# A down projection in parts: 24 of its 44 inner tiles as seven products of sums, partial results accumulated in DRAM

## The chip, the cores and the metric

The kernel runs on one core of a Trainium2 chip. The metric is the device time in microseconds (us) of one execution; less is better. The engines are called by their names in the profile as well: TensorE (PE; its weight loads are PEld), VectorE (DVE), ScalarE (ACT), GpSimd (POOL) and SyncE (SP), whose queue issues most DMAs.

## What is computed

One step of a decoder layer for 512 prompt tokens and 64 sample tokens, 576 together. Cut to what matters here:

```
x = x + concat(A, B) @ w_out                       # 2048 -> 2048
up = rmsnorm(x, g_ffn) @ w_up                      # 2048 -> 2 x 5632
upc = causal_dwconv(up_ext, w_dw_f, b_dw_f)        # width 3, along the tokens
x = x + (silu(upc[..., :D_FF]) * upc[..., D_FF:]) @ w_down     # 5632 -> 2048
gate = sigmoid(rmsnorm(x, g_ple) @ w_ple_gate)
x = x + gate * (p @ w_ple_proj)
```

All is float32. The down projection is the product with `w_down`: 44 inner tiles of 128 channels (`NF`), 16 output tiles (`KT`).

## The kernel before

Channels lie on the 128 partitions and tokens along the free axis, as two halves of 288 (`HT`). A float32 product is made of three matmuls in the format `fp32r`: every operand is split into a high part `h` and a rest `l`, and `wh x bh + wh x bl + wl x bh` is summed in PSUM. So a tile of weights (128x128) against all 576 tokens is six matmuls of 288 columns (L862, L864, L866).

Weights come in one stream, `wstream`, in the order in which TensorE wants them: units of 8 tiles, 512 KB each, in five buffers `raw`. A piece is 4 tiles (128x512). `prepare` splits a piece: ScalarE copies the high part into `wh` (L249), VectorE subtracts it and leaves the rest in `wl` (L250), four buffers each, up to four pieces ahead of TensorE.

The up projection (`up_pair`, one pair of output tiles for each of 44 `j`) is already computed by seven products of sums (Strassen's scheme in Winograd's form): instead of eight block products of (output row) x (inner half) x (token half) it takes seven, in the order of `PRODS`, with sums of weight pieces made on VectorE (`add_up`, L209), sums of operands made once (`sum_in`), and the seven results put together by subtractions from PSUM (L718) and copies on ScalarE. A piece there feeds 12 matmuls, in a plain product 24.

Each pair's result then goes through a convolution of width 3, SiLU and a product (`conv_f`, `hidden`), mostly on VectorE: that gives the hidden tile `j`. For the 22 `j` in `SOON` this is done beside the next pair of the up projection and the hidden tile is stored in DRAM (`hidd`); for the 22 in `LATER` the raw result is stored (`upd`) and the convolution is done beside the down projection. Such side work is dealt out from the queues `todo` and `urgent` after every fourth tile, at a rate (`state["rate"]`) that the phases set; the scheduler of the tile framework then orders the instructions of each engine.

The down projection runs over four chunks of 12, 10, 16 and 6 inner tiles (`CHUNKS`, in `ORDER`). In each, the first three output tiles are computed together and the other 13 one after the other; the three accumulators (`acc`, two PSUM banks each) rotate. At the end of an output's chunk VectorE adds its accumulator to `x1r`, the running sum in SBUF, which is loaded from DRAM (`x1d`) when the down projection begins (L810, L905). In the last chunk the sum is normalised, split and squared for the next product (`split_in`, `add_square`). Each chunk's hidden tiles are fetched beside the chunk before (`fetch_hidden`), the first chunk's at the end of the up projection (L721 to L724).

Of the kernel before, what the change touches and what calls it, by code (L numbers as in the profile page):

```python
# [39 lines left out]
SOON = sorted([*range(2, NF - 3, 2), NF // 4, 3 * NF // 4])  # L40
LATER = [j for j in range(NF) if j not in SOON]
ORDER = SOON + LATER
CHUNKS = [12, 10, 16, 6]

COMING = [12, 22, 34, 44, 44]
RATE_D = [0.3, 1.6, 1.0, 0.0]
# [17 lines left out]
def plan():  # L64
# [46 lines left out]
    at = 0  # L111
    for c, n in enumerate(CHUNKS):
        js = ORDER[at : at + n]
        at += n
# [34 lines left out]
def trunk_kernel(ctx: ExitStack, tc: tile.TileContext, A, O):  # L149
# [28 lines left out]
    HID = [x for n in (2, 3, 4, 0, 1) for x in by_kind[n]] + SPARE  # L178
    RES2 = by_kind[5] + by_kind[6]
# [48 lines left out]
    def prepare(s):  # L228
# [17 lines left out]
        else:  # L246
            h = tl([P, SUB * P], HID[32 + 2 * spare], f"wh{s}", dt=F32R)
            l = tl([P, SUB * P], HID[33 + 2 * spare], f"wl{s}", dt=F32R)
# [327 lines left out]
    def sum_in(q):  # L576

        box = {}
        return [(1.5, lambda: add_in(q, box)), (1.1, lambda: first_in(q, box)), (1.4, lambda: last_in(q, box))]

    def add_in(q, box):
        g = []
        for n in range(2):
            g.append(tmp(f"xg{2 * q + n}"))
            nc.scalar.activation(g[n], res[2 * q + n], AF.Copy, scale=v("g_ffn", 2 * q + n))
        e, o = g
        ta, tb = tmp(f"ta{q}"), tmp(f"tb{q}")
        nc.vector.tensor_tensor(out=ta[:, 0, :], in0=e[:, 0, :], in1=e[:, 1, :], op=ALU.subtract)
        nc.vector.tensor_tensor(out=ta[:, 1, :], in0=o[:, 1, :], in1=ta[:, 0, :], op=ALU.add)
        nc.vector.tensor_tensor(out=tb[:, 0, :], in0=e[:, 1, :], in1=o[:, 1, :], op=ALU.subtract)  # L590
        nc.vector.tensor_tensor(out=tb[:, 1, :], in0=o[:, 0, :], in1=ta[:, 1, :], op=ALU.subtract)
        box.update(e=e, o=o, ta=ta, tb=tb)

    def first_in(q, box):
        e = box["e"]
# [474 lines left out]
```

## Time and profile before

| | |
|---|---|
| median of 3 runs | 2446.71 us (2446.13 to 2448.26) |
| the profiled execution, its own time | 2449.88 us |
| its span in the trace | 2448.1 us |
| PE busy | 2422.2 us, 99% |
| PEld busy | 2412.7 us, 99% |
| DVE busy | 1804.1 us, 74% |
| ACT busy | 1115.7 us, 46% |
| POOL busy | 92.5 us, 4% |
| matmuls | 18200 |
| mean granted TensorE clock | 0.996 of full speed |

The span is that of the instructions in the trace; the execution's own time lies 1.8 us above it. The busy share of an engine is the time in which it had an instruction under way; matmuls are pipelined, so a busy PE may still be short of its best pace.

### The profile page before, as it was taken

The numbers are of one execution on the slowest core, as the hardware profiler recorded it, in microseconds if no ns is written. First come the engines' busy times: TensorE is split into PE (matmuls) and PEld (weight loads), VectorE is DVE, ScalarE is ACT, GpSimd is POOL, SyncE is SP. The second block draws the span as 40 slices with busy tenths as digits, with TensorE's granted clock in tenths as the row PEclk, the third lists the DMA queues.
The fourth block names the chain that finished last, engine by engine and source line by source line (L and its number), as shares of the span: only waits on it lengthen the run. The fifth ranks groups of instructions, "written<-read, shape, count | busy, mean of one in ns | idle before, by whom it ended". The sixth has DMA issues, their size and how long they took to land.

```text
span 2448.1 us, 45485 instructions
## 1 busy us (share of the span) xinstructions
PE 2422.2 (99%) x18200; PEld 2412.7 (99%) x18200; DVE 1804.1 (74%) x3155; ACT 1115.7 (46%) x2072; POOL 92.5 (4%) x175
## 2 busy tenths in 40 slices
PE   9999999999999999999999999999999999999997
PEld 8999999999999999999999999999999999999997
DVE  7877788885888879888888798886459762254445
ACT  6444445433665545445445454454235431243334
POOL 1000000000200000000000000000000000000000
PEclk9999999999999999999999999999999999999998
DMA  6332222333563333433333434357334432222322
GB/s 238 95 84 83 85 84 84 123 107 101 193 216 118 115 121 99 132 111 110 118 118 115 121 98 132 112 172 275 101 110 148 133 120 79 86 87 78 121 96 93
DMA packets 106196, 294.71 MB, mean 120 GB/s; under 512 B 23568, under 2 KB 27792, under 8 KB 105984
## 3 DMA queue, kind: packets, MB, share of 16 engines
q1 hardware_dynamic: 96096, 259.20, 33.8%
q0 software_dynamic: 9744, 32.60, 3.8%
q8 instruction: 143, 2.34, 0.4%
q14 instruction: 69, 0.57, 0.1%
q10 hardware_dynamic: 144, 0.01, 0.0%
HBM read 255.43 MB, written 36.32 MB: 119 GB/s over the span
## 4 chain that ended last, share of the span: by engine, by line
PE 95%; issue 2%; DMA 1%; DVE 1%; ACT 1%; POOL 0%; SPq 0%; DVEq 0%; POOLq 0%
PE acc L862 18%; PE acc L866 18%; PE acc L864 18%; PE acc_up L729 13%; PE acc_up L730 13%; PE acc_up L731 13%; POOL x1d L901 0%; DMA x<-in_xT 0%; PE vps L512 0%; DMA xs<-x1d 0%; PE mps L550 0%; PE acc L936 0%; PE acc L935 0%; PE acc L937 0%; DMA hq<-hidd 0%
## 5 line engine op out<-in xcount | busy, mean ns | idle before, releaser
L249 ACT ACTIVATE wh<-raw 128x512 fp32r<-128x512 f32 x792 | 500.2, 632 | 945.1 <-PE acc L864 676.8
L250 DVE TENSOR_TENSOR wl<-raw,wh 128x512 fp32r<-128x512 f32 x792 | 543.5, 687 | 362.1 <-ACT wh L249 357.7
L729 PE MATMUL acc_up<-sx,wh 128*128 128x288 f32 x2464 | 726.8, 295 | 0.1
L731 PE MATMUL acc_up<-sx,wl 128*128 128x288 f32 x2464 | 726.6, 295 | 0.2 <-DVE wl L250 0.2
L730 PE MATMUL acc_up<-sx,wh 128*128 128x288 f32 x2464 | 726.5, 295 | 0.0
L729 PEld LDWEIGHTS acc_up<-sx,wh 128*128 128x128 f32 x2464 | 463.8, 188 | 0.8 <-ACT sq L303 0.3
L730 PEld LDWEIGHTS acc_up<-sx,wh 128*128 128x128 f32 x2464 | 463.8, 188 | 0.1
L731 PEld LDWEIGHTS acc_up<-sx,wl 128*128 128x128 f32 x2464 | 463.0, 188 | 0.4 <-DVE wl L250 0.4
L862 PE MATMUL acc<-xh,wh 128*128 128x288 f32 x1984 | 427.2, 296 | 5.7 <-ACT wh L249 5.3
L864 PE MATMUL acc<-xl,wh 128*128 128x288 f32 x1984 | 423.6, 295 | 0.3 <-DVE xl L291 0.3
L866 PE MATMUL acc<-xh,wl 128*128 128x288 f32 x1984 | 423.5, 294 | 0.0
L862 PEld LDWEIGHTS acc<-xh,wh 128*128 128x128 f32 x1984 | 318.4, 188 | 7.9 <-ACT wh L249 5.3
L864 PEld LDWEIGHTS acc<-xl,wh 128*128 128x128 f32 x1984 | 319.2, 188 | 0.8 <-DVE xl L291 0.6
L866 PEld LDWEIGHTS acc<-xh,wl 128*128 128x128 f32 x1984 | 318.1, 188 | 0.3 <-issue 0.3
L862 PE MATMUL acc<-hh,wh 128*128 128x288 f32 x1408 | 301.2, 295 | 2.3 <-DVE ua L718 1.8
L866 PE MATMUL acc<-hh,wl 128*128 128x288 f32 x1408 | 301.3, 295 | 0.0
L864 PE MATMUL acc<-hl,wh 128*128 128x288 f32 x1408 | 301.1, 295 | 0.0
L862 PEld LDWEIGHTS acc<-hh,wh 128*128 128x128 f32 x1408 | 226.6, 188 | 2.9 <-DVE ua L718 2.1
L864 PEld LDWEIGHTS acc<-hl,wh 128*128 128x128 f32 x1408 | 226.7, 189 | 0.0
L866 PEld LDWEIGHTS acc<-hh,wl 128*128 128x128 f32 x1408 | 226.3, 188 | 0.0
L249 ACT ACTIVATE wh<-sy 128x512 fp32r<-128x512 f32 x176 | 111.7, 635 | 160.6 <-PE acc_up L730 156.8
L445 DVE SCALAR_TENSOR_TENSOR cv<-ep,vec,cv 128x512 f32<-128x512 f32 x240 | 178.8, 745 | 0.0
(192 smaller groups left out, 2184.0 us busy)
## 6 DMA issues: line engine op xcount, KB each, us to landing
raw<-in_wstream SPq DMA_DIRECT2D x395, 512.0 KB
uz<-upd SPq DMA_DIRECT2D x44, 288.0 KB
upd<-ub POOLq DMA_DIRECT2D x22, 288.0 KB, 2.6
upd<-ua POOLq DMA_DIRECT2D x22, 288.0 KB, 2.4
hidd<-hp POOLq DMA_DIRECT2D x22, 288.0 KB, 3.9
hq<-hidd SPq DMA_DIRECT2D x22, 288.0 KB
x<-in_xT SPq DMA_DIRECT2D x16, 288.0 KB
xr<-in_xT SPq DMA_DIRECT2D x16, 288.0 KB
```

The costliest lines, as they stand in the source:

```text
L249: nc.scalar.activation(h, src, AF.Copy)
L250: nc.vector.tensor_tensor(out=l, in0=src, in1=h.bitcast(F32), op=ALU.subtract)
L445: tc.keep_in_program_order(nc.vector.scalar_tensor_tensor(out=cp, in0=halves(ep[:, k : k + SEQ]), scalar=w, in1=cp, op0=ALU.mult, op1=ALU. ...
L729: nc.tensor.matmul(place[prod], wh, bh, start=k == 0 and not on, stop=False, skip_group_check=on)
L730: nc.tensor.matmul(place[prod], wh, bl, start=False, stop=False, skip_group_check=on)
L731: nc.tensor.matmul(place[prod], wl, bh, start=False, stop=k == KT // 2 - 1, skip_group_check=on)
L862: nc.tensor.matmul(accs[n][:, h, :HT], wh, bh[:, h, :], start=st, stop=False)
L864: nc.tensor.matmul(accs[n][:, h, :HT], wh, bl[:, h, :], start=False, stop=False)
L866: nc.tensor.matmul(accs[n][:, h, :HT], wl, bh[:, h, :], start=False, stop=sp)
```

## The change

24 of the 44 inner tiles of the down projection go through the seven products as well. The down projection has seven parts (`DOWN`): plain ones with 6, 5, 5 and 4 inner tiles, and between them three parts of 8 inner tiles each by seven products (`quad1`, `quad3`, `quad5`). In such a part a block (`down_four`) is four output tiles by eight inner tiles: output row x inner half x token half, for two pairs of output tiles and four pairs of inner tiles. The weight sums are those of the up projection (`add_up`), the operand sums are made as `sum_in` makes them (`sum_steps`, in `fetch_two`).

Results no longer stay in SBUF between the parts: a plain part's accumulator is copied by ScalarE into one of four staging tiles and GpSimd adds it to `x1d` in DRAM by an accumulating DMA (L1000, L1001); a block's four result tiles are added in halves of the tokens, eight DMAs a block (L761). `x1d` is read back for the last part alone (L903). `LATER` is cut from 22 `j` to 8, so 36 pairs of the up projection have their convolution beside the next pair.

```diff
-SOON = sorted([*range(2, NF - 3, 2), NF // 4, 3 * NF // 4])
-LATER = [j for j in range(NF) if j not in SOON]
+LATER = [0, 1, NF // 3, NF // 2, 2 * NF // 3, NF - 3, NF - 2, NF - 1]
+SOON = [j for j in range(NF) if j not in LATER]
 ORDER = SOON + LATER
-CHUNKS = [12, 10, 16, 6]
-
-COMING = [12, 22, 34, 44, 44]
-RATE_D = [0.3, 1.6, 1.0, 0.0]
+DOWN = [(False, SOON[:6]), (True, SOON[6:14]), (False, LATER[:4] + SOON[14:15]), (True, SOON[15:23]),
+        (False, LATER[4:7] + SOON[23:25]), (True, SOON[25:33]), (False, LATER[7:] + SOON[33:])]
+
+RATE_D = [1.9, 0.0, 1.9, 0.0, 1.6, 0.0, 0.0]
...
+    for c, (summed, js) in enumerate(DOWN):
+        if summed:
+            for m in range(0, KT, 4):
+                add(f"quad{c}", "w_down", range(m, m + 4), js)
+            continue
...
+        elif phase.startswith("quad"):
+            w, m = outs[0]
+            for row, odd in ((0, 0), (1, 0), (1, 1), (0, 1)):
+                tiles += [(w, k, m + 2 * pair + row) for pair in range(2) for k in ks[odd::2]]
+            pieces += [(n // UNIT, prod, half) for prod in PRODS for half in range(2)]
...
+    def fetch(c):
+
+        summed, js = DOWN[c]
+        if summed:
+            return [f for n in range(0, len(js), 2) for f in fetch_two(c, js[n], js[n + 1])]
+        return [f for j in js for f in fetch_hidden(j, grab(c, 2))]
+
+    def fetch_two(c, i, j):
+        box = []
+
+        def load():
+            for m in (i, j):
+                box.append(tmp(f"hq{m}"))
+                nc.sync.dma_start(box[-1], hid_d[m])
+
+        return [(0.0, load)] + sum_steps(lambda: box, grab(c, 7), f"h{i}", sums_h.setdefault(c, []))
...
+    def down_four(c, ms):
+
+        ones, sixes, fives = (psum.tile([P, 2, 512], F32, tag="acc", name=f"acc{c}_{ms[0]}_{n}", bufs=3)
+                              for n in range(3))
+        place = {1: ones, 2: ones, 6: sixes, 7: sixes, 4: sixes, 5: fives, 3: fives}
+        o11, o12, o21, o22, first, u = (tl([P, 2, HT], STAGE[n], f"o{c}_{ms[0]}_{n}") for n in range(6))
+
+        def out(o, row, half):
+            for pair in range(2):
+                nc.gpsimd.dma_start(x1_d[ms[2 * pair + row]][:, half, :], o[:, pair, :], accum_op=ALU.add)
+
+        for prod in PRODS:
+            on = prod not in (1, 6, 5)
+            for pair in range(2):
+                dst = place[prod][:, pair, :HT]
+                for k, two in enumerate(sums_h[c]):
+                    wh, wl = weights()
+                    bh, bl = two[prod]
+                    end = k == len(sums_h[c]) - 1
+                    nc.tensor.matmul(dst, wh, bh, start=k == 0 and not on, stop=False, skip_group_check=on)
+                    nc.tensor.matmul(dst, wh, bl, start=False, stop=False, skip_group_check=on)
+                    nc.tensor.matmul(dst, wl, bh, start=False, stop=end, skip_group_check=on)
+                deal()
+            acc = place[prod][:, :, :HT]
+            if prod == 1:
+                nc.scalar.activation(first, acc, AF.Copy)
+            if prod == 6:
+                sub(u, acc, first)
+            if prod == 7:
+                sub(o22, acc, first)
+                sub(o22, o22, fives[:, :, :HT])
+                out(o22, 1, 1)
+            if prod == 2:
+                nc.scalar.activation(o11, acc, AF.Copy)
+                out(o11, 0, 0)
+            if prod == 4:
+                sub(o21, acc, first)
+                out(o21, 1, 0)
+            if prod == 3:
+                sub(o12, acc, u)
+                out(o12, 0, 1)
...
-                state["rate"] = 1.1
-                for i in ORDER[: COMING[0]]:
-                    urgent.extend(fetch_hidden(i, slot_of(i)))
+                state["rate"] = 0.8
+                urgent.extend(fetch(0))
...
-                nc.vector.tensor_tensor(out=res[m], in0=acc[:, :, :HT], in1=res[m], op=ALU.add)
-                if phase == n_down:
+                if phase != n_down:
+                    a = tl([P, 2, HT], STAGE[m % 4], f"o{phase}_{m}")
+                    nc.scalar.activation(a, acc[:, :, :HT], AF.Copy)
+                    nc.gpsimd.dma_start(x1_d[m], a, accum_op=ALU.add)
+                else:
+                    nc.vector.tensor_tensor(out=res[m], in0=acc[:, :, :HT], in1=res[m], op=ALU.add)
```

How the instructions stand on the engines is shown at three places; the number behind an underscore at a name's end is a buffer's.

TensorE, before, inside the first chunk of the down projection (`acc117_0` to `_2` are its first three accumulators, `hh` and `hl` hidden tiles, `x2` the two halves of the tokens): the four tiles of weight piece 818.

```order
L862 MATMUL acc117_2_19963<-hh6_19760,wh818_19910 128x288 x2
L864 MATMUL acc117_2_19963<-hl6_19761,wh818_19910 128x288 x2
L866 MATMUL acc117_2_19963<-hh6_19760,wl818_19911 128x288 x2
L862 MATMUL acc117_0_19961<-hh8_19766,wh818_19910 128x288 x2
L864 MATMUL acc117_0_19961<-hl8_19767,wh818_19910 128x288 x2
L866 MATMUL acc117_0_19961<-hh8_19766,wl818_19911 128x288 x2
```

TensorE now, at the start of the first part by seven products (`acc1_0_0` is the accumulator `ones` of its first block, `sxh8`, `sxh10` the operand sums of the pairs of hidden tiles 8, 9 and 10, 11):

```order
L771 MATMUL acc1_0_0_21216<-sxh8_2_20255,wh840_21123 128x288
L772 MATMUL acc1_0_0_21216<-sxh8_2_20255,wh840_21123 128x288
L773 MATMUL acc1_0_0_21216<-sxh8_2_20255,wl840_21124 128x288
L771 MATMUL acc1_0_0_21216<-sxh10_2_20338,wh840_21123 128x288
L772 MATMUL acc1_0_0_21216<-sxh10_2_20338,wh840_21123 128x288
L773 MATMUL acc1_0_0_21216<-sxh10_2_20338,wl840_21124 128x288
```

A tile of weights has three matmuls there, and twice as many pieces pass for the same number of matmuls.

VectorE, before, where the up projection hands over to the down projection (`ua43` is the last result of the up projection, `hl` the rests of hidden tiles, `wl817` to `wl819` weight pieces of the first chunk):

```order
L250 TENSOR_TENSOR wl817_19881<-raw276_19661,wh817_19880 128x512
L683 TENSOR_TENSOR hl28_20065<-hq28_20062,hh28_20064 128x576
L683 TENSOR_TENSOR hl30_20101<-hq30_20098,hh30_20100 128x576
L250 TENSOR_TENSOR wl818_19911<-raw277_19845,wh818_19910 128x512
L683 TENSOR_TENSOR hl32_20135<-hq32_20132,hh32_20134 128x576
L718 TENSOR_TENSOR ua43_19606<-acc_up2_7937,uu43_19609 128x288
```

VectorE now, where the first part by seven products hands over to the second plain part (`o1_12_2` and `o1_12_1` are the last two results of its last block, `sxh20` and `sxh23` operand sums of the next such part, `wl897` and `wl898` weight pieces of the plain part):

```order
L616 TENSOR_TENSOR sxh20_6_22412<-hq21_22370,sxh20_5_22411 128x576
L750 TENSOR_TENSOR o1_12_2_22025<-acc1_12_1_22021,o1_12_4_22027 128x576
L261 TENSOR_TENSOR wl897_22246<-raw304_22080,wh897_22245 128x512
L616 TENSOR_TENSOR sxh23_6_22477<-hq24_22463,sxh23_5_22476 128x576
L261 TENSOR_TENSOR wl898_22264<-raw305_22220,wh898_22263 128x512
L616 TENSOR_TENSOR sxh23_4_22475<-tah23_22465,sxh23_3_22474 128x576
L750 TENSOR_TENSOR o1_12_1_22024<-acc1_12_2_22022,o1_12_5_22028 128x576
```

The last subtraction of a part stands behind two weight pieces and two operand sums, as `ua43` stood behind hidden tiles. That place occurs after the first and the second such part; after the third only weight pieces stand there.

GpSimd, before, from the end of the up projection to the end of the program: stores of the up projection's results, and rows of the convolution's history.

```order
L749 DMA upd87_225<-ub43_19607 128x576
L748 DMA upd43_224<-ua43_19606 128x576
L624 MEMSET hist5_21967 128x12x2
L671 DMA out_ffn_conv<-last3_16371 128x216
L624 MEMSET hist6_22582 128x12x2
```

GpSimd now, from the last outputs of the first plain part (`odown0`) into the first block (`o1_0`):

```order
L1001 DMA x1d14_142<-odown0_14_21169 128x576
L1001 DMA x1d15_143<-odown0_15_21213 128x576
L761 DMA x1d1_129<-o1_0_3_21222 128x288
L761 DMA x1d3_131<-o1_0_3_21222 128x288
L761 DMA x1d0_128<-o1_0_0_21219 128x288
L761 DMA x1d2_130<-o1_0_0_21219 128x288
```

GpSimd has 144 accumulating DMAs there, one after the other, where it had almost nothing to do.

## Rows read from the trace of the kernel before

**Rows 1.** The page: the span, and busy time, share and instructions of each engine.

```profile
span 2448.1 us, 45485 instructions
...
PE 2422.2 (99%) x18200; PEld 2412.7 (99%) x18200; DVE 1804.1 (74%) x3155; ACT 1115.7 (46%) x2072; POOL 92.5 (4%) x175
```

**Rows 2.** Waits of PE: total us, times, longest us.

```profile
PE acc L862 <- ACT wh L249: 5.8, 2, 5.3
...
PE acc L862 <- DVE ua L718: 1.8, 1, 1.8
```

**Rows 3.** Windows: stretch, length, busy us of PE, PEld, DVE, ACT, POOL; PEclk, DMA.

```profile
1015.00:1616.20 601.20, 601.20 (x4538) 601.20 (x4537) 507.27 (x880) 298.59 (x567) 22.94 (x44) 1.00 0.37 118
...
2000.00:2060.00 60.00, 60.00 (x456) 60.00 (x455) 16.00 (x25) 12.04 (x19) 0.00 (x0) 1.00 0.25 80
...
1660.50:2224.30 563.80, 561.52 (x4228) 560.87 (x4227) 321.73 (x520) 212.12 (x435) 3.76 (x10) 1.00 0.39 122
...
1661.00:1700.00 39.00, 37.16 (x269) 36.92 (x268) 21.19 (x35) 14.65 (x30) 0.54 (x1) 0.96 0.82 290
```

**Rows 4.** Groups by line, PE, 1660.5 to 2224.3; L864 and L866 alike.

```profile
L862 PE MATMUL acc<-hh,wh 128*128 128x288 f32 x1408 | 301.2, 295 | 2.3 <-DVE ua L718 1.8 <-ACT wh L249 0.4
```

**Rows 5.** Timeline of PE: start us, us, instruction, count [idle before, releaser].

```profile
1664.09 0.53 PE L862 MATMUL acc<-hh,wh 128*128 128x288 f32 x2 [1.84 <-DVE ua L718]
...
1665.36 0.69 PE L864 MATMUL acc<-hl,wh 128*128 128x288 f32 x2
1665.84 0.69 PE L866 MATMUL acc<-hh,wl 128*128 128x288 f32 x2
...
1982.75 0.50 PE L862 MATMUL acc<-hh,wh 128*128 128x288 f32 x2 [0.44 <-ACT wh L249]
1983.09 0.42 PE L864 MATMUL acc<-hl,wh 128*128 128x288 f32 x2
1983.35 0.43 PE L866 MATMUL acc<-hh,wl 128*128 128x288 f32 x2
```

**Rows 6.** The chain that ended last, 1655 to 1665 us: start, us, what.

```profile
1655.56 5.48 DMA hq<-hidd
...
1663.66 0.38 DVE ua L718
```

**Rows 7.** Windows, columns as in rows 3: three pairs with a convolution, one without.

```profile
926.00:948.20 22.20, 22.20 (x169) 22.20 (x169) 20.65 (x38) 12.27 (x26) 0.54 (x1) 1.00 0.35 113
948.20:970.50 22.30, 22.30 (x171) 22.30 (x170) 20.77 (x38) 12.37 (x26) 1.21 (x3) 1.00 0.33 108
970.50:992.80 22.30, 22.30 (x171) 22.30 (x170) 20.75 (x38) 12.37 (x26) 1.08 (x2) 1.00 0.40 121
992.80:1015.00 22.20, 22.20 (x169) 22.20 (x169) 16.36 (x28) 9.42 (x17) 0.54 (x1) 1.00 0.37 111
```

**Rows 8.** Groups by line, DVE: busy us, mean ns | idle before, releasers.

```profile
L250 DVE TENSOR_TENSOR wl<-raw,wh 128x512 fp32r<-128x512 f32 x792 | 543.5, 687 | 362.1 <-ACT wh L249 357.7
...
L905 DVE TENSOR_TENSOR x1r<-acc,x1r 128x576 f32<-128x576 f32 x64 | 48.1, 755 | 59.8 <-PE acc L866 59.7
...
L604 DVE TENSOR_TENSOR sx<-ta,sx 128x576 fp32r<-128x576 f32 x8 | 6.0, 753 | 0.0
```

**Rows 9.** Groups by line, ACT, columns as in rows 8.

```profile
L249 ACT ACTIVATE wh<-raw 128x512 fp32r<-128x512 f32 x792 | 500.2, 632 | 945.1 <-PE acc L864 676.8 <-PE acc_up L730 209.8 <-ACT ue L638 16.6
...
L911 ACT ACTIVATE pa<-acc 128x576 f32<-128x576 f32 x16 | 10.1, 657 | 2.5 <-DMA pjd<-pa 1.8 <-PE acc L866 0.6
```

**Rows 10.** DMA queues (packets, MB, share of 16 engines); issues (KB, median us to landing).

```profile
q1 hardware_dynamic: 96096, 259.20, 33.8%
q0 software_dynamic: 9744, 32.60, 3.8%
...
pjd<-pa POOLq DMA_DIRECT2D x16, 288.0 KB, 3.6
...
out_conv_a_sample<-es POOLq DMA_DIRECT2D x8, 120.0 KB, 6.7
```

More of the change, by code (lines that the diff above doesn't have):

```diff
@@ L175, in trunk_kernel @@
     by_kind = {n: [TAGS[7 * q + n] for q in range(KT // 2)] for n in range(7)}
-    HID = [x for n in (2, 3, 4, 0, 1) for x in by_kind[n]] + SPARE
-    RES2 = by_kind[5] + by_kind[6]
+    HOMES = deque(x for n in (2, 3, 4, 0, 1, 5, 6) for x in by_kind[n])
+    STAGE = [HOMES.pop() for _ in range(6)]
+    LAST_W, LAST_Y = [], SPARE
     def load_unit(u):
@@ L576, in sum_in @@
     def sum_in(q):
-        box = {}
[L579 to L592, printed above, removed]
@@ L594, in first_in @@
-    def first_in(q, box):
-        e = box["e"]
-        t = box["t"] = [tl([P, 2, HT], by_kind[n][q], f"sx{q}_{n}", dt=F32R) for n in range(7)]
-        nc.scalar.activation(t[2][:, 0, :], e[:, 0, :], AF.Copy)
-        nc.vector.tensor_tensor(out=t[2][:, 1, :], in0=e[:, 0, :], in1=t[2][:, 0, :].bitcast(F32), op=ALU.subtract)
-        halves_in(t, ((3, box["ta"]),))
-    def halves_in(t, pairs):
-        for n, x in pairs:
-            nc.scalar.activation(t[n], x, AF.Copy)
-            nc.vector.tensor_tensor(out=t[n + 1], in0=x, in1=t[n].bitcast(F32), op=ALU.subtract)
@@ L674, in hidden, with grab, split_hidden @@
         return [(0.8, both)]
-    def slot_of(j):
-        return ORDER.index(j) % (len(HID) // 2)
-    def split_hidden(j, slot, p):
-        h = tl([P, 2, HT], HID[2 * slot], f"hh{j}", dt=F32R)
-        l = tl([P, 2, HT], HID[2 * slot + 1], f"hl{j}", dt=F32R)
+    homes = {}
+    def grab(c, n):
+        got = [HOMES.popleft() for _ in range(n)]
+        homes.setdefault(c, []).extend(got)
+        return got
+    def split_hidden(j, tags, p):
+        h = tl([P, 2, HT], tags[0], f"hh{j}", dt=F32R)
+        l = tl([P, 2, HT], tags[1], f"hl{j}", dt=F32R)
         nc.scalar.activation(h, p, AF.Copy)
@@ L766, in trunk_kernel @@
         first_of.setdefault(phase, gi)
-    down0, n_down = "down0", f"down{len(CHUNKS) - 1}"
-    x_tags = [(HID[2 * k], HID[2 * k + 1]) for k in range(KT)]
+    n_down = f"down{len(DOWN) - 1}"
+    x_tags = []
     pj = {}
@@ L805, in trunk_kernel @@
             rows_of(ORDER[0])
-        if phase == "down0" and prev == "up":
+        if phase[:4] in ("down", "quad") and phase != prev:
+            c = int(phase[4:])
             settle(lambda: not (urgent or todo))
-            for m in range(KT):
-                res[m] = tl([P, 2, HT], RES2[m], f"x1r_{m}")
-                nc.sync.dma_start(res[m], x1_d[m])
-        if phase.startswith("down") and phase != prev:
-            c = int(phase[4:])
-            settle(lambda: not todo)
-            state["credit"], state["rate"] = 0.0, RATE_D[c]
-            for j in ORDER[COMING[c] : COMING[c + 1]]:
-                todo.extend(fetch_hidden(j, slot_of(j)))
+            state["credit"], state["rate"] = 0.0, RATE_D[c]
+            if c:
+                HOMES.extend(homes.pop(c - 1))
+            for a in {0: (1, 2), 2: (3, 4), 4: (5, 6)}.get(c, ()):
+                todo.extend(fetch(a))
+            if phase == n_down:
+                got = [HOMES.popleft() for _ in range(KT)]
+                for m in range(KT):
+                    res[m] = tl([P, 2, HT], got[m], f"x1r_{m}")
+                    nc.sync.dma_start(res[m], x1_d[m])
+                free = [*HOMES, *STAGE]
+                x_tags.extend(zip(free[::2], free[1::2]))
+                LAST_W.extend(homes[c])
         if phase == "ple" and prev != "ple":
@@ L832, in trunk_kernel @@
             up_pair(j)
+            continue
+        if phase.startswith("quad"):
+            down_four(int(phase[4:]), [m for _, m in outs])
             continue
```

66 lines of the change are left out of this document (45 added, 21 removed).

## Prediction

> **What bounds the kernel now.** I read the busy shares first: TensorE is busy for 2422.2 of 2448.1 us [rows 1]. The waits of TensorE come next: the longest is 5.3 us, at the program's start, and in the stretch that changes the longest is 1.8 [rows 2], so no other engine sets the time over any long stretch. What an edit is worth is therefore the number of matmuls it takes away, times their pitch, less the new waits. The pitch comes from counts over stretches. A matmul's record is 295 ns long, so a stretch counts two that only reach over its edge. The window 1015.0 to 1616.2 us holds 27 pairs of the up projection: 601.20 us over 4538 - 2 = 4536 = 27 x 168 matmuls, 132.5 ns each [rows 3]. The plain down projection, 2000 to 2060 us, gives 60 / 454 = 132.2 ns [rows 3].
>
> The down projection holds 3 x 1408 = 4224 matmuls [rows 4] and lasts 563.8 us, from 1660.5 to 2224.3 [rows 3]. At 132.2 ns it would last 558.4, so 5.4 us are lost in it. Most of that is the hand-over from up: 39 us hold 267 matmuls, 35.3 us of work, so 3.7 us are lost there [rows 3]. The timeline shows how: TensorE waits 1.84 us for VectorE's last subtraction `ua`, and behind the wait a pair of matmuls takes 0.48 us (1665.36 to 1665.84) where it takes 0.26 elsewhere (1983.09 to 1983.35) [rows 5]. The granted clock of that window is 0.96 [rows 3]; the slow pairs are the 1.2 GHz level. `ua` was late because it stood in VectorE's queue behind splits of hidden tiles, and the chain goes back from them to a load of 5.48 us [rows 6].
>
> **What is removed.** A tile of weights against all 576 tokens is six matmuls. Four output tiles by eight inner tiles are 32 tiles, 192 matmuls, when plain; as seven products of four inner pairs, two output pairs and three matmuls they are 168. There are 3 x 4 such blocks: 288 matmuls fewer, each with its weight load. After: 20 inner tiles x 16 x 6 = 1920 plain matmuls at 132.2 ns (253.8 us) and 2016 others at the up projection's 132.5 (267.2 us), since they have its form: 521.0 us against 558.4. Term 1: **-37.4 us**. If both forms ran at 132.2 it would be -38.1.
>
> **What is added, and what covers it.**
>
> *VectorE and ScalarE in the new blocks.* Each block takes 14 splits and 8 sums of 128x512 at 687 ns, and 5 subtractions of 128x576 from PSUM at 755 [rows 8]: 18.9 us of 22.3. The up projection's heaviest pairs have VectorE busy for 20.75 us and stall nothing [rows 7], so 0; without that cover the excess over 22.3 would fall on TensorE. ScalarE has 14 x 0.632 + 2 x 0.66 = 10.2 us [rows 9]: 0. The operand sums (12 pairs of hidden tiles at about 4.5 us of VectorE: three 753 ns subtractions [rows 8] and five of half size, my estimate at 450 ns) go beside the 254 us of plain parts, which need 80 splits, 55 us; plenty is free.
>
> *Convolutions moved into the up projection.* 36 of 44 pairs now carry their convolution there, before 22: 14 more. A pair with one has VectorE busy for 20.7 us, one without for 16.4 [rows 7]: 14 x 4.3 = 60 us more, in place of the same work in the down projection. The trace already has three heavy pairs in a row (j = 10, 11, 12 are all in `SOON`): VectorE is busy 20.65, 20.77 and 20.75 us in them and TensorE the whole of each [rows 7]. The order of VectorE's instructions in a heavy pair doesn't change. So 0; the bound above is in the rivals.
>
> *Results through DRAM.* In the plain parts ScalarE copies the sum out (the same copy, `pa`, took 657 ns [rows 9]) where VectorE added it; GpSimd then issues an accumulating DMA: 48 of 288 KB, and 96 of 144 KB from the blocks, 28.3 MB. No row shows an accumulating DMA. Below: the plain store of such a copy lands in 3.6 us, the slowest store here in 6.7 [rows 10]. What can wait for it is ScalarE, which needs one of four staging tiles back. The tightest case is the fifth output of a part with five inner tiles: outputs 0 to 2 end 0.79 us apart and the next two 3.97 apart, so 9.5 us pass from the end of output 0 to that of output 4, less 0.66 for the copy and 0.5 for the issue: some 8.3 us; later it is 15.9. Behind a waiting copy stand ScalarE's weight splits. Up to 8 us of landing cost nothing; above, see the rivals. I take 5 us, nearest to the plain store, so 0. Occupancy: loads move 259.20 MB in 33.8% of the span, 313 GB/s at full share, and GpSimd's stores 32.60 MB in 3.8%, 350 GB/s [rows 10]. The new down projection loads 46.1 MB of weights and 68 tiles (20.1 MB): 211 us. One pass over 28.3 MB is 81 us. Of 521 us that is 56%; the engines are full only if an accumulate costs 3.8 such passes.
>
> The Trainium skill's page "DMA: Bandwidth & Descriptors" (Rules for kernel authors) says that an accumulating DMA reads its destination and writes it later, and that the next access must wait for its semaphore. By that rule an accumulate is about two passes; the share would be 72% and the sum the same. No run so far shows it.
>
> *Loads of `x1`.* Sixteen loads that ran at the hand-over now stand in the last block part on SP's queue, in fours, each behind the accumulates of its tiles. Behind the last two only one weight load of the last part waits, needed some 40 us later: 0.
>
> *Last part with four inner tiles.* An output takes 3.17 us; VectorE's add (755), normalising split, square sum and 1 weight split come to about 3.0 by their durations, less where they overlap. Tight but below: 0, bound +2.
>
> **The hand-overs: term 2.** A plain part's third accumulator is the bank of the product that finished last. TensorE comes to it after two tiles, 12 x 0.132 = 1.59 us; VectorE's subtraction takes 0.755. Alone it is in time. After the first and second block part the order puts two sums and two weight splits between the previous subtraction and this one; if one of each is still ahead, 0.755 + 0.753 + 0.687 = 2.2 us, 0.6 us late. Two of these: +1.2. The third has only weight splits ahead: 0. The old hand-over from up keeps its form, with about as many loads of hidden tiles ahead of it but without the 16 loads of `x1` beside them. Between 0 and its present 3.7 us I take half: -1.9. Term 2: **-0.7 us**. Bounds: -3.7 (no hand-over costs anything) to +11.1 (four at 3.7).
>
> **Sum.** -37.4 - 0.7 = -38.1. The profiled execution took 2449.88 us (span 2448.1), so it would be 2411.8; the median of the runs is 3.2 lower, 2446.71, and gives 2408.6. I say **2409 us**, its own range 2405 to 2420.
>
> **Rivals.**
>
> *Every hand-over pays as the old one did.* For it: VectorE's order, above; and the slow pairs after the wait. Against: a wait of 0.44 us at 1982 us was followed by pairs of 0.26 [rows 5], so a short one costs itself alone. Four at 3.7: -37.4 + 11.1 = -26.3, **2420 us**. The Trainium skill's "TensorE: Matmul & The Clock Gate" (What's actually happening) has the throttled clock as the default that activity releases; by that rule many small waits could add up to more than their length. The trace agrees for the 1.84 us wait and not for the 0.44 one.
>
> *VectorE becomes the bound in the up projection.* A heavy pair leaves 22.27 - 20.75 = 1.5 us. With twelve in a row, if waits between VectorE and ScalarE come to 2.0 us a pair, 0.5 x 36 = 18 us are lost: **2427 us**. Against: three in a row show no loss.
>
> *The accumulates land too late (slower).* Four staging tiles and a landing of L us let a plain part finish an output each (L + 1.2) / 4 us; it wants 3.97 (32 outputs) or 4.76 (16). The loss is 12 (L + 1.2) - 203 us: it begins near L = 15 and eats the whole gain at L = 19. At 22 us: +75, **2484 us**. Against: the slowest store takes 6.7; for: no accumulate has been seen.
>
> *It is a wash.* Losses of 33 to 43 us from small waits in all seven parts, over 5 us each: nothing in the profile looks like it.
>
> **Chances.** Forecast 0.74; all hand-overs 0.08; VectorE 0.06; better than 2405, with every stall gone, 0.04; late accumulates 0.05; a wash 0.03. The range 2404 to 2422 holds the forecast, the hand-over rival and part of the better case, 0.84. A measurement of this kernel tells 0.2%, 5 us, from no change: faster 0.92, same 0.03, slower 0.05.
>
> **What would show it.** Right: 17912 matmuls in all, at 132 to 133 ns; TensorE full from 1016 to 1616 us, VectorE near 20.7 us in each heavy pair; waits below 1 us behind the block parts; accumulates landing in under 8 us, and no wait of ScalarE's copies for them. Wrong: waits of the up matmuls for `wl`; copies waiting for DMAs; stretches of 240 ns matmuls at each part.

## The result, and the profile after

The changed kernel takes 2410.49 us (median of four runs, 2409.45 to 2413.74) where the kernel before took 2447.34 beside it: a ratio of 0.9852, 95% interval 0.9835 to 0.9869. The prediction was 2409, range 2404 to 2422. In a later comparison it was 2411.78 against 2448.81, 0.985 (0.9836 to 0.9863). The profiled execution took 2409.46 us, 40.4 less than that of before; the medians lie 36.9 us apart, since the profiled execution of before was 2.5 us above its median and this one 1.0 below.

The page, beside [rows 1]: span, then busy time, share and instructions of each engine.

```profile
span 2407.8 us, 45825 instructions
...
PE 2382.8 (99%) x17912; PEld 2373.9 (99%) x17912; DVE 1928.2 (80%) x3407; ACT 1212.1 (50%) x2240; POOL 208.5 (9%) x305
```

TensorE is as full as before, with 288 matmuls fewer. To see where the 40.4 us between the two profiles are, I cut both spans at the first matmul of the up projection, of the down projection and of the gate product:

| stretch, us | before | after | difference |
|---|---|---|---|
| ahead of the up projection | 678.43 | 677.91 | -0.5 |
| up projection | 982.07 | 981.88 | -0.2 |
| down projection | 563.64 | 525.58 | -38.1 |
| behind it | 223.96 | 222.38 | -1.6 |

Inside the down projection I took the distances between the starts of matmuls that follow one another. Without those over 200 ns the mean is 132.36 ns before and 132.58 after; what the long ones have over 133 ns adds up to 4.5 us before and 3.75 after. So 4224 x 132.36 = 559.1 became 3936 x 132.58 = 521.8, **-37.3 us from the matmuls, -0.8 from lost time**.

The windows after, columns as in [rows 3]: 27 pairs of the up projection, a heavy pair, the start of the down projection, the second part by seven products, the whole down projection.

```profile
1015.00:1616.20 601.20, 601.20 (x4539) 601.20 (x4538) 545.88 (x971) 324.35 (x648) 18.85 (x38) 1.00 0.36 114
926.00:948.20 22.20, 22.20 (x170) 22.20 (x169) 20.64 (x38) 12.34 (x25) 0.54 (x1) 1.00 0.41 115
...
1661.00:1700.00 39.00, 37.39 (x280) 36.91 (x279) 32.77 (x60) 23.70 (x54) 6.59 (x8) 1.00 0.86 220
...
1891.30:1980.30 89.00, 89.00 (x673) 89.00 (x672) 72.14 (x118) 45.10 (x75) 26.76 (x31) 1.00 0.72 155
...
1660.00:2185.00 525.00, 522.02 (x3934) 521.34 (x3933) 384.47 (x626) 267.40 (x474) 125.41 (x147) 1.00 0.78 178
```

In the 27 pairs VectorE does 38.6 us more than in [rows 3] (545.88 against 507.27) and TensorE is still never idle; a heavy pair looks as in [rows 7]. In the part by seven products VectorE is busy for 72.14 / 4 = 18.0 us a block and TensorE for the whole of it. The last window's DMA share is 0.78.

The waits of TensorE, columns as in [rows 2]:

```profile
PE rps L1057 <- ACT sq L1048: 1.6, 1, 1.6
PE acc L955 <- ACT odown L1000: 1.4, 1, 1.4
PE acc L771 <- DVE o L750: 1.4, 1, 1.4
...
PE acc L955 <- DVE ua L750: 0.2, 1, 0.2
```

The wait for `ua`, 1.84 us in [rows 2], is down to 0.2. Two waits of 1.4 us are new, and neither is at a place that the prediction named. The first stands in the first plain part. The timeline of TensorE there, columns as in [rows 5]:

```profile
1674.34 0.43 PE L959 MATMUL acc<-hh,wl 128*128 128x288 f32 x2
1676.16 0.53 PE L955 MATMUL acc<-hh,wh 128*128 128x288 f32 x2 [1.39 <-ACT odown L1000]
1676.53 0.42 PE L957 MATMUL acc<-hl,wh 128*128 128x288 f32 x2
1676.79 0.43 PE L959 MATMUL acc<-hh,wl 128*128 128x288 f32 x2
```

And ScalarE's at the same time:

```profile
1673.93 0.20 ACT L665 ACTIVATE last<-ue 128x2 f32<-128x2 f32 x1 [2.00 <-DVE ue L661]
...
1674.19 0.87 ACT L667 ACTIVATE uc<-ue,vec 128x592 f32<-128x592 f32 x1
1674.96 0.61 ACT L260 ACTIVATE wh<-raw 128x512 fp32r<-128x512 f32 x1
1675.48 1.71 ACT L1000 ACTIVATE odown<-acc 128x576 f32<-128x576 f32 x3
```

ScalarE stood 2.00 us at a convolution step that waited for VectorE; behind it were two more steps of the convolution, a weight split and then the copies of the first three outputs, whose last matmul begins near 1674.5. The pairs of matmuls behind this wait are 0.26 us apart: no half clock follows here, as it did in [rows 5].

The second wait stands in the third part by seven products. VectorE there:

```profile
2103.16 0.69 DVE L220 TENSOR_TENSOR sx<-raw,raw 128x512 f32<-128x512 f32 x1 [3.77 <-DMA raw<-in_wstream]
2103.77 0.68 DVE L261 TENSOR_TENSOR wl<-raw,wh 128x512 fp32r<-128x512 f32 x1
2104.37 0.69 DVE L220 TENSOR_TENSOR sx<-raw,raw 128x512 f32<-128x512 f32 x1
2104.97 0.75 DVE L750 TENSOR_TENSOR o<-acc,o 128x576 f32<-128x576 f32 x1
```

The subtraction of the fourth product, for which TensorE waits, stands behind the sums of weights for the next block, and those wait for a load. The chain of waits (start us, us, what) gives that load, and SP's work ahead of it: a load of `x1` for the last part.

```profile
2096.59 0.32 SPq L903
...
2097.01 6.06 DMA raw<-in_wstream
```

The DMA queues and issues, columns as in [rows 10], and GpSimd's three largest groups by line:

```profile
q0 software_dynamic: 29360, 56.79, 11.6%
...
x1d<-odown POOLq DMA_DIRECT2D x48, 288.0 KB, 5.5
x1d<-o POOLq DMA_DIRECT2D x96, 144.0 KB, 5.0
```

```profile
L761 POOL DMA_DIRECT2D x1d<-o x96 | 82.9, 1068 | 188.2 <-DVE o L750 169.3 <-DVE wl L261 17.4 <-issue 0.7
L1001 POOL DMA_DIRECT2D x1d<-odown x48 | 40.8, 873 | 154.7 <-ACT odown L1000 136.4 <-ACT ue L659 14.2 <-DMA hist<-in_histF 4.2
L837 POOL DMA_DIRECT2D hidd<-hp x36 | 19.5, 540 | 746.9 <-DVE hp L688 746.9
```

The accumulates land in 5.0 to 5.5 us, and GpSimd spends 0.87 to 1.07 us on one where a plain store takes it 0.54.

### The profile page after: what moved, and what is told of

Read it like the earlier page. It is cut to its first block, busy times and chain, and to the rows that moved or that the text cites. A ratio compares the mean times of both kernels' runs of the same rounds, so it can differ in the third digit from the quotient of the medians.

```text
span 2407.8 us, 45825 instructions
## 1 busy us (share of the span) xinstructions
PE 2382.8 (99%) x17912; PEld 2373.9 (99%) x17912; DVE 1928.2 (80%) x3407; ACT 1212.1 (50%) x2240; POOL 208.5 (9%) x305
## 3 DMA queue, kind: packets, MB, share of 16 engines
q0 software_dynamic: 29360, 56.79, 11.6%
## 4 chain that ended last, share of the span: by engine, by line
PE 94%; issue 2%; DMA 1%; DVE 1%; ACT 1%; POOL 0%; SPq 0%; DVEq 0%; ACTq 0%; POOLq 0%
PE acc L955 14%; PE acc L957 14%; PE acc L959 14%; PE acc_up L815 13%; PE acc_up L814 13%; PE acc_up L816 13%; PE acc L771 4%; PE acc L773 4%; PE acc L772 4%; DMA hq<-hidd 0%; POOL x1d L994 0%; PE acc L1034 0%; PE acc L1032 0%; PE acc L1033 0%; DMA x<-in_xT 0%
## 5 line engine op out<-in xcount | busy, mean ns | idle before, releaser
L260 ACT ACTIVATE wh<-sy 128x512 fp32r<-128x512 f32 x224 | 142.2, 635 | 206.4 <-PE acc_up L815 155.1
L771 PE MATMUL acc<-sxh,wh 128*128 128x288 f32 x672 | 198.3, 295 | 1.4 <-DVE o L750 1.4
L773 PE MATMUL acc<-sxh,wl 128*128 128x288 f32 x672 | 198.1, 295 | 0.0
L772 PE MATMUL acc<-sxh,wh 128*128 128x288 f32 x672 | 198.1, 295 | 0.0
L261 DVE TENSOR_TENSOR wl<-sy,wh 128x512 fp32r<-128x512 f32 x224 | 153.2, 684 | 50.1 <-ACT wh L260 49.9
L672 DVE SCALAR_TENSOR_TENSOR uc<-ue,vec,uc 128x592 f32<-128x592 f32 x176 | 145.6, 828 | 23.6 <-ACT uc L667 23.5
L955 PE MATMUL acc<-hh,wh 128*128 128x288 f32 x640 | 136.9, 295 | 1.6 <-ACT odown L1000 1.4
```

Source lines behind the costliest of these rows:

```text
L260: nc.scalar.activation(h, src, AF.Copy)
L261: nc.vector.tensor_tensor(out=l, in0=src, in1=h.bitcast(F32), op=ALU.subtract)
L771: nc.tensor.matmul(dst, wh, bh, start=k == 0 and not on, stop=False, skip_group_check=on)
L772: nc.tensor.matmul(dst, wh, bl, start=False, stop=False, skip_group_check=on)
L773: nc.tensor.matmul(dst, wl, bh, start=False, stop=end, skip_group_check=on)
L955: nc.tensor.matmul(accs[n][:, h, :HT], wh, bh[:, h, :], start=st, stop=False)
```

## The experiments

**The moved convolutions alone.** The kernel before, with the lists of the changed one:

```diff
-SOON = sorted([*range(2, NF - 3, 2), NF // 4, 3 * NF // 4])
-LATER = [j for j in range(NF) if j not in SOON]
+LATER = [0, 1, NF // 3, NF // 2, 2 * NF // 3, NF - 3, NF - 2, NF - 1]
+SOON = [j for j in range(NF) if j not in LATER]
```

> The kernel before with only its two lists of pairs changed: 36 pairs have their convolution beside the next pair of the up projection, 8 beside the down projection, which stays plain. Theory (TensorE bounds, VectorE has room in every pair): no change, 2445 to 2449 us beside 2447; the up projection keeps 132.5 ns a matmul, and at most the hand-over to the down projection, 3.7 us lost before, changes. Rival (the moved convolutions cost time in the up projection, which the changed kernel hides in its gain): up to 18 us slower, 2465 us, with waits of up matmuls for wl. Other rival (the down projection was slowed by its convolutions): faster by 3 us or more.

2450.25 us against 2448.05, ratio 1.0008 (0.9999 to 1.0018). The up projection takes 982.07 us, as before, and its window is full:

```profile
1015.00:1616.20 601.20, 601.20 (x4538) 601.20 (x4538) 546.06 (x969) 324.36 (x647) 18.89 (x38) 1.00 0.36 114
```

So the moved convolutions are free where they went, and where they came from they had cost nothing either. The median is a little above the 2445 to 2449 that I expected, and the difference is not clear of noise. In the trace the down projection is 1.2 us longer, with a new wait:

```profile
PE acc L862 <- DVE x1r L905: 1.8, 1, 1.8
```

**All parts plain.** In the changed kernel:

```diff
-DOWN = [(False, SOON[:6]), (True, SOON[6:14]), (False, LATER[:4] + SOON[14:15]), (True, SOON[15:23]),
+DOWN = [(False, SOON[:6]), (False, SOON[6:14]), (False, LATER[:4] + SOON[14:15]), (False, SOON[15:23]),
...
-        (False, LATER[4:7] + SOON[23:25]), (True, SOON[25:33]), (False, LATER[7:] + SOON[33:])]
+        (False, LATER[4:7] + SOON[23:25]), (False, SOON[25:33]), (False, LATER[7:] + SOON[33:])]
```

> The changed kernel with its three parts by seven products made plain: 18200 matmuls again, but the seven parts, the accumulates in DRAM (112 of 288 KB in place of 48 and 96 halves) and the moved convolutions stay. Theory (the gain is the 288 matmuls and nearly nothing else): 2410.5 + 37.4, less the 1.4 us wait in the third block part, plus or minus 2: 2445 to 2449 us, the time of before. Rival (parts and accumulates cost something that the 37 us hide): over 2452 us. Rival (parts help by themselves, as through a lighter hand-over): under 2443.

2447.89 us against 2448.05, ratio 0.9998 (0.9989 to 1.0007). The first theory holds: parts, accumulates and moved convolutions together are worth nothing; the seven products are worth everything. Its down projection has no gap over 300 ns but one of 1.6 us, and no wait for `ua` at all: from 1640 us on eight loads of hidden tiles are issued ahead of it, the last at 1651 us, where there were twelve, the last at 1657, and no `x1` is loaded there.

**Two parts by seven products.** The middle one of the three is plain:

```diff
-        (True, SOON[15:23]),
+        (False, SOON[15:23]),
```

> The changed kernel with the middle one of its three parts by seven products made plain: 96 matmuls more. Theory: a third of term 1 is given back, 12.5 us, 2421 to 2425 us. Rival (the gain comes from a place of its own, such as the first part's hand-over): the time stays within 5 us of 2410, or goes up by 20 or more.

2426.89 us, 16.4 over the changed kernel's 2410.49, and 2 above what I expected. 96 matmuls at 132.5 ns are 12.7 of it. The long distances in its down projection add up to 7.6 us against 3.75, 3.9 more. Its waits in the down projection:

```profile
PE acc L955 <- ACT odown L1000: 3.3, 2, 1.8
PE acc L771 <- DVE o L750: 1.7, 1, 1.7
...
PE acc L955 <- DVE o L750: 1.6, 1, 1.6
```

The copies are late twice: at 1677 us behind the convolution step, as above, and at 1844 us behind a copy for an operand sum, which waits for VectorE as well:

```profile
1842.78 0.69 ACT L615 ACTIVATE sxh<-tah 128x576 fp32r<-128x576 f32 x1 [1.42 <-DVE tah L608]
```

The wait in the last block part is there too, and, at 1831 us, one at the hand-over from the first block part to the plain part behind it: the kind that the prediction priced at 0.6 us, and that the changed kernel does not show. Here VectorE stood at a weight split that waited for ScalarE, with a split of a hidden tile and the last subtraction behind it:

```profile
1829.56 0.69 DVE L261 TENSOR_TENSOR wl<-raw,wh 128x512 fp32r<-128x512 f32 x1 [2.02 <-ACT wh L260]
```

The 96 matmuls give back their share; small waits come and go with each re-ordering.

**Plain stores.**

```diff
-nc.gpsimd.dma_start(x1_d[m], a, accum_op=ALU.add)
+nc.gpsimd.dma_start(x1_d[m], a)
```

and the same for the blocks.

> The changed kernel with plain stores in place of the 144 accumulating DMAs; the sum over the parts is left out, so that the last part adds its share to the last thing stored. Theory (landings and traffic are covered): 2408 to 2412 us; GpSimd's queue falls from 11.6% of the engines' span to about 7% (28.3 MB at some 350 GB/s in place of some 143), landings from 5 to about 3.6 us, and the wait of 1.4 us in the third block part, where the loads of x1 stand behind accumulates on SP's queue, shrinks or goes. Rival (the traffic of the accumulates slows TensorE's weights everywhere): faster by over 4 us, under 2406.

2409.55 us, ratio 0.9844 (0.983 to 0.9859), 0.9 us under the changed kernel's median: the accumulates cost a microsecond or so at most. Queues and landings:

```profile
q0 software_dynamic: 17072, 56.79, 6.4%
...
x1d<-odown POOLq DMA_DIRECT2D x48, 288.0 KB, 3.3
x1d<-o POOLq DMA_DIRECT2D x96, 144.0 KB, 3.1
```

For the same bytes the queue has 17072 packets, not 29360, and takes 6.4% of the engines' span, not 11.6. That is 125 us less; the plain stores of 28.3 MB are half of the 154 us that are left, 77. So an accumulate takes (125 + 77) / 77 = 2.6 store passes. The stretch from 1665 to 2150 us, in which this queue carries little else, says the same directly: its packets took 41.6% of 485 us, 202 us, against 15.8%, 77 us. The wait at 2104 us is gone, while the one behind the copies is 0.3 us longer; VectorE waits 1.32 us for the same load, not 3.77:

```profile
2102.28 0.69 DVE L220 TENSOR_TENSOR sx<-raw,raw 128x512 f32<-128x512 f32 x1 [1.32 <-DMA raw<-in_wstream]
```

**Every accumulate twice.** The second goes to a second set of tensors:

```diff
-                nc.gpsimd.dma_start(x1_d[...][:, half, :], o[:, pair, :], accum_op=ALU.add)
+                for d in (x1_d, x2_d):
+                    nc.gpsimd.dma_start(d[...][:, half, :], o[:, pair, :], accum_op=ALU.add)
```

> The changed kernel with every accumulating DMA sent a second time to a second set of 16 tensors in DRAM (a copy of x1, stored beside it, 16 stores more), which nothing reads. By the two traces an accumulate takes of the DMA engines about 2.6 times what the plain store takes: GpSimd's queue 11.6% of 2408 us with accumulates, 6.4% with stores, so 125 us more over 28.3 MB, 202 us in all. The engines' mean share in the down projection was 0.78 of 525 us. Theory (the share is a real occupancy, and the engines become the bound when it is over 1): 0.78 + 202 / 525 = 1.16, so the down projection takes some 0.16 x 525 = 85 us longer, 2480 to 2510 us, with TensorE waiting for weights. Rival (the share holds much waiting; there is room for twice the accumulates): under 2420 us.

One run of 2456.21 us, between the two: the down projection takes 569.1 us, 43.5 more, half of what I expected.

```profile
1662.00:2231.00 569.00, 537.25 (x3938) 533.71 (x3937) 384.40 (x625) 266.85 (x475) 251.96 (x291) 0.97 0.95 214
```

The share rises to 0.95, and 0.95 x 569 - 0.78 x 525 = 131 us were added for the second set, not 202. The share adds up the times of packets, and these overlap: from 1836 to 1905 us it is 1.10. So a sum of shares overstates what a transfer will cost. Landings went from 5.5 and 5.0 to 9.4 and 7.9 us:

```profile
x1d<-odown POOLq DMA_DIRECT2D x48, 288.0 KB, 9.4
...
x1d<-o POOLq DMA_DIRECT2D x96, 144.0 KB, 7.9
```

That full DMA engines are all of it is not shown. Some of TensorE's waits end with late loads (10.2 us for a hidden tile at 1870 us, 7.1 for weights at 1893), but the longest distance, 5.2 us at 2029, ends with a copy whose staging tile was held by two accumulates, one after the other (9.2 and 11.3 us). GpSimd's records of the halves also grew, from 1.07 to about 2 us.

**One staging tile for the plain parts.**

```diff
-                    a = tl([P, 2, HT], STAGE[m % 4], f"o{phase}_{m}")
+                    a = tl([P, 2, HT], STAGE[0], f"o{phase}_{m}")
```

> The changed kernel with one staging tile in place of four for the outputs of the plain parts; the blocks keep their own. By the prediction's sum for late accumulates an output then takes landing + 1.2 us: 48 x (5.5 + 1.2) - 203 = +119 us, 2530 us (2500 to 2550), with ScalarE's copies waiting for accumulates and TensorE for ScalarE. Rival (the landing in the profile holds waiting behind other transfers and is shorter when one accumulate is out at a time, as 3.3 for a plain store): 48 x 4.5 - 203 = +13, about 2425. Other rival (ScalarE's wait hides behind the split weights that are four pieces ahead): under 2415.

One run of 2482.40 us: 72 slower, where I expected 119. The mechanism is the one named; ScalarE's copies wait for landings, and TensorE for the copies:

```profile
ACT odown L1000 <- DMA x1d<-odown: 152.6, 44, 5.6
```

```profile
PE acc L955 <- ACT odown L1000: 33.5, 33, 3.1
```

```profile
x1d<-odown POOLq DMA_DIRECT2D x48, 288.0 KB, 4.3
```

With one accumulate out at a time it lands in 4.3 us, not 5.5, and 48 x (4.3 + 1.2) - 203 = 61. That is near the 72 in size, but not in place: what the long distances have over 133 ns adds up to 75.1 us, 47.2 in the plain parts and 27.9 in the block parts, which the sum does not count. There TensorE waits most for `wh` (7.5 us), split behind copies that still wait, as at 1934 us. Some 7 us of the whole are clock: 68 distances of about 240 ns in five unbroken rows of 10 to 18, the first of them in a window (1676 to 1686 us) with a granted clock of 0.83.

**Loads of `x1` issued by GpSimd.**

```diff
-                    nc.sync.dma_start(res[m], x1_d[m])
+                    nc.gpsimd.dma_start(res[m], x1_d[m])
```

> The changed kernel with the 16 loads of x1 for the last part issued by GpSimd behind its accumulates, not by SP ahead of weight loads; the bytes are the same. Theory (the 1.4 us wait at 2104 us came because SP stood at loads of x1 that waited for accumulates, with a weight load behind them): that wait is gone, the third block part holds 1344/2 = 672 matmuls at 132.6 ns without a gap, 2407 to 2410 us. Rival (the engines were too full there for the weight load, whoever issues the others): a gap of about 1.4 us stays in that part.

One run of 2411.14 us, and my theory falls: the wait is shorter, but there.

```profile
2107.07 0.37 PE L771 MATMUL acc<-sxh,wh 128*128 128x288 f32 x1 [0.79 <-DVE o L750]
```

SP's timeline shows the weight load going out at 2098.17 us with nothing ahead of it, as late as in the other two kernels (2097.01 with the loads of `x1` ahead, 2097.95 with plain stores); its buffer does not come free sooner.

```profile
2098.17 3.35 SPq L200 DMA_DIRECT2D raw<-in_wstream  x2
```

```profile
2104.35 0.69 DVE L220 TENSOR_TENSOR sx<-raw,raw 128x512 f32<-128x512 f32 x1 [3.18 <-DMA raw<-in_wstream]
```

It is its travel that differs: VectorE takes the data up 6.2 us after the issue here (2098.17 to 2104.35), and 6.1 in the changed kernel, against 4.3 with plain stores (2097.95 to 2102.28). The windows of the changed kernel ahead of that load show why:

```profile
2083.50:2093.50 10.00, 10.00 (x78) 10.00 (x77) 9.28 (x15) 4.56 (x8) 6.47 (x8) 1.00 1.00 188
2093.50:2104.50 11.00, 11.00 (x84) 10.77 (x82) 4.77 (x8) 4.32 (x8) 0.00 (x0) 1.00 0.80 232
```

For ten microseconds the share is 1.00, and then loads of `x1` and of weights travel together.

**The old hand-over without its loads of `x1`.** In the kernel before, each `x1r` is loaded as its output's first chunk begins:

```diff
-        if phase == "down0" and prev == "up":
-            settle(lambda: not (urgent or todo))
-            for m in range(KT):
+        if phase == "down0":
+            for _, m in outs:
                 res[m] = tl([P, 2, HT], RES2[m], f"x1r_{m}")
                 nc.sync.dma_start(res[m], x1_d[m])
```

> The kernel before with each x1r loaded when its output's first chunk begins, not all 16 at the start of the down projection. The prediction laid part of the old hand-over's 3.7 us on these loads, beside the loads of hidden tiles. Theory: the wait for ua falls from 1.84 us to under 0.7 and no pairs of 0.48 us follow; about 3 us faster, 2443 to 2446. Rival (ua is late because of the splits of 12 hidden tiles ahead of it on VectorE, whatever else is loaded): the wait stays between 1.2 and 2.2 us with slow pairs behind, 2446 to 2450.

The wait falls from 1.8 to 1.1, between my theory and the rival, and one distance of 240 ns follows where 15 did:

```profile
PE acc L863 <- DVE ua L718: 1.1, 1, 1.1
```

The down projection takes 561.55 us, 2.1 less, 0.7 of it in the wait and 1.5 in the slow distances; the one time, 2448.41 against 2446.73 beside it, can't tell that, and is where the rival put it. That the loads of `x1` carried those 2.1 us is not shown. In the run with the moved convolutions alone all 16 stay in place, and yet TensorE's wait for `ua` is hardly longer, with one slow distance behind it:

```profile
PE acc L862 <- DVE ua L718: 1.3, 1, 1.3
```

And the load in the chain to `ua`, 5.48 us in [rows 6], took 5.95 with only the first three loads of `x1` behind it. So the old hand-over varies by 2 us, mostly with the clock behind it, even where these loads stay, and their share is open.

**Loads of `x1` kept inside the last part.** One output ahead of their use:

```diff
+        if phase == n_down:
+            for m in range(outs[-1][1] + 2 if outs[0][1] else 4):
+                if m < KT and m not in x1_in:
+                    x1_in.add(m)
+                    res[m] = tl([P, 2, HT], got[m], f"x1r_{m}")
+                    tc.keep_in_program_order(nc.sync.dma_start(res[m], x1_d[m]))
```

> The changed kernel with the 16 loads of x1 kept in SP's order inside the last part, one output ahead of their use, so that they no longer run in the third block part. Theory (in that part the DMA engines are full for some 10 us, accumulates and loads of x1 together, so that a weight load lands 2 us late and VectorE's sum of it holds up the subtraction queued behind it): the gap of 1.66 us at 2104 us goes, TensorE has no wait in the third block part, 2407 to 2410 us. Rival (accumulates alone fill the engines there): a gap of 1 us or more stays at that place. Risk: the first loads come too late for the last part, with TensorE waiting at its first outputs for VectorE's additions.

2409.32 us, one run. The wait in the third block part is gone (VectorE waits 0.47 us for the load there, not 3.77), and TensorE's windows are full:

```profile
2085.00:2095.00 10.00, 10.00 (x78) 10.00 (x77) 8.13 (x13) 4.59 (x8) 5.21 (x7) 1.00 1.06 172
2095.00:2106.00 11.00, 11.00 (x85) 11.00 (x85) 8.10 (x13) 4.32 (x8) 0.22 (x1) 1.00 0.44 110
```

The accumulates alone fill the engines too (1.06), but what comes behind them, 0.80 before, is 0.44.

**Copies ahead of convolution steps.**

```diff
+        def behind():
+            with tc.issue_after(state["copy"]):
+                scaled()
...
-        return [(0.75, scaled), (0.7, lambda: tap(1)), (0.7, lambda: tap(0))]
+        return [(0.75, behind if m % NF in LATER else scaled), (0.7, lambda: tap(1)), (0.7, lambda: tap(0))]
...
-                    nc.scalar.activation(a, acc[:, :, :HT], AF.Copy)
+                    state["copy"] = nc.scalar.activation(a, acc[:, :, :HT], AF.Copy).ins
```

> The changed kernel with the convolution steps of the plain parts put on ScalarE behind the last output's copy, not ahead of it. Theory (the wait of 1.4 us at 1674 us came because ScalarE stood at a convolution step that waited for VectorE, with the copies of the first three outputs behind it): the wait falls to 0.3 us or less, 2407.5 to 2410 us. Rival (the copies are late because of their own time, 3 x 0.66 us one after the other): a wait of about 1 us stays.

2408.60 us, one run; no wait is left at 1674 us, the one in the third block part stays (1.6 us), and there is another of 0.6 us at 2081, where VectorE also waits for a load.

**Both edits, and the changed kernel again.**

> Both edits of the two runs beside this one in the changed kernel. Theory: the two waits of 3.1 us together are all that is left to win in the down projection beside the pitch; 2406 to 2409 us, ratio to before about 0.9840, ratio to the changed kernel about 0.9988. Rival (one wait moves to the next place in its queue): 2409 to 2412, no difference to the changed kernel.

> The changed kernel itself, for the comparison with the run beside it: 2409 to 2413 us, and how far one profile of it lies from the other; the two waits of 1.4 us should be there again if they belong to the order and not to chance.

Both edits: 2407.59 us (2406.32 to 2408.14), ratio to before 0.983 (0.9816 to 0.9843). The changed kernel beside it: 2411.78 (2410.66 to 2414.36). The five and four runs don't overlap; 4.2 us, and this version beats both kernels. Its down projection holds 3936 matmuls in 521.8 us, not one distance over 200 ns:

```profile
1661.50:2183.00 521.50, 521.50 (x3936) 521.50 (x3935) 383.98 (x625) 267.93 (x474) 125.39 (x147) 1.00 0.78 179
```

The changed kernel's second profile has both waits again, so they belong to the order, and they are longer: 2.1 and 1.5 us, and half clock behind the first. The first stands in every run with block parts that keeps ScalarE's order (1.7 to 2.4 us between the starts of the matmuls on either side). A third, of 0.7 us at 1887 us, is in the second profile alone. A window of ten microseconds there:

```profile
1676.00:1686.00 10.00, 7.92 (x48) 7.69 (x47) 6.84 (x12) 6.82 (x16) 2.69 (x3) 0.83 0.83 182
```

Its down projection loses 6.5 us in all, against 3.75 in the first profile.

## Why the prediction was right

**Term 1** was -37.4 and came out at -37.3. With all parts plain the whole gain is gone; with both waits removed the down projection is nothing but 3936 x 132.57 ns = 521.8 us, where the prediction had 521.0. Its pitches were too low by 0.7 us in the kernel before and by 0.8 in the changed one, which cancels.

**Term 2** was -0.7 and came out at -0.8, but for other reasons; its parts were mis-sized and cancelled. The old hand-over gave back 3.3 of its 3.7 us, not half (0.4 us of a gap is left). The prediction gave the credit to the 16 loads of `x1` and took the loads of hidden tiles to be about as many as before; from 1640 us to `ua` there are six, not twelve. Which of the two counts is not shown. The two new hand-overs, +1.2 in the sum, cost nothing in the changed kernel (at the first, the last subtraction begins 1828.06 us, 0.6 us after the block's last matmul began, and TensorE wants the bank at 1829.21), but 1.6 us once with two parts, where VectorE had stood 2.02 us at a split that waited for ScalarE. In place of these came two waits, 1.55 and 1.53 us with what surrounds them, together +3.1, at places that were priced at zero. And the wait of 0.44 us that [rows 5] show at 1982 us went with the old order. That these come to -0.8 is luck: with the second profile of the changed kernel, which loses 6.5 us, term 2 would be +2.0. The time was right because the matmuls are nearly all of it.

**The zero for ScalarE's copies** rested on staging tiles and landings alone. The order on ScalarE's queue was not looked at: convolution steps that wait for VectorE stand ahead of the copies. Moving the copies ahead of them removes the wait.

**The zero for loads of `x1`** failed in its reason, that behind them only a weight load of the last part waits. They run through the third block part, where accumulates fill the engines; a weight load lands 2 us late, and VectorE's queue has a subtraction behind the sum that needs it. My first account, SP's queue, fell to the run with GpSimd's loads.

**VectorE and the moved convolutions** were right: 38.6 us more in 27 pairs, where the two lists put 9 more convolutions (9 x 4.3 = 38.7), and no loss in the up projection with them alone. In the blocks VectorE is busy for 18.0 us, 18.9 being taken, and ScalarE for 45.10 / 4 = 11.3, not 10.2, and TensorE lost nothing in the second such part. Nor did the last part lose anything: in the first profile no distance over 200 ns stands behind 2106 us.

**Accumulates** were right in what they do to the time: they land in 5.0 to 5.5 us, 5 being taken, and the copies wait for matmuls only, as ScalarE's waits show:

```profile
ACT odown L1000 <- PE acc L959: 23.5, 22, 2.0
```

Their occupancy was not: 2.6 store passes, by the times of their packets. The Trainium skill's "DMA: Bandwidth & Descriptors" (Rules for kernel authors) says that an accumulate reads its destination and writes it later. The prediction's two passes were an estimate from that; the runs say more. The share of the down projection was 0.78, not 56%, and 1.00 for ten microseconds at a stretch, where the prediction looked at the mean alone. The formula for late accumulates gave 61 of 72 us with the landing that one staging tile shows, and left out the blocks (its loss begins at L = 15.7, not near 15).

**The late tail.** 1.6 us came behind the down projection: TensorE's wait for `sq` there was 3.3 us before and 1.6 after. It was 2.6 with all parts plain and 2.7 with the moved convolutions alone. No run was made for its cause.

Of the rivals, VectorE as the bound and late accumulates are excluded by runs. Hand-overs that all pay are excluded by the trace of the changed kernel, where three of the four cost nothing and the first 0.4; yet its second profile, with half clock behind one wait, shows what that rival saw.

## What to carry to other kernels

Where one engine is full, count its instructions and their pitch first: that gave 37.3 of 38.1 us here. Then read, for each result that it waits for, the whole queue of the engine that delivers it, for instructions ahead that themselves wait for a third engine or a load; pricing each addition by its own duration finds none of these. A transfer that is hidden on average may not be where two bursts meet: look at the DMA share in windows of ten microseconds, and move what isn't urgent to a quiet stretch.

## What the hardware showed that I had not expected

The packets of an accumulating DMA to DRAM took 2.6 times the time of those of a plain store of the same bytes. There were 1.7 times as many packets on its queue, GpSimd spent 0.87 to 1.07 us on one in place of 0.54, and it landed 1.9 to 2.2 us later.

Whether the clock falls behind a wait was not settled by the wait's length alone. Slow pairs followed a gap of 2.14 us in the kernel before, of 2.06 with the moved convolutions and of 2.37 in the second profile of the changed kernel; none followed one of 2.09 with two parts, of 2.02 with plain stores, of 2.36 at the same place with GpSimd's loads and of 2.65 with one staging tile. The Trainium skill's "TensorE: Matmul & The Clock Gate" (What's actually happening) has throttling as the default and activity as what releases it; these runs show both outcomes for nearly the same gap, and no run here tells what decides.
